# Short experts' fold matmuls move into the Else arm of the branch around the third passes (one core, mixture-of-experts trunk)

## The chip, the cores and the metric

The kernel runs on one core of one Trainium2 chip. The metric is the device time of one execution in microseconds (us), lower is better. The figure before is 1691.68 us, the median of 3 runs (1690.11 to 1696.17).

## What is computed

The reference is a two-layer trunk over 256 tokens of width 1024: an RWKV-7 time mix with a dense feed-forward part, then an attention layer with a mixture of experts (MoE), and a final norm. The change lies in the mixture of experts alone:

```python
# 8 experts, the best 2 of them per token; x is [256, 1024], w_gu[e] is [1024, 2*3584], w_down[e] is [3584, 1024]
gate, up = jnp.split(x @ w_gu[e], 2, axis=-1)
y_e = (jax.nn.silu(gate) * up) @ w_down[e]        # for the tokens routed to expert e
out[token] += gate_weight[token, e] * y_e
```

All is float32. The weights of one expert are 44 MB, and all 8 experts are read.

## The kernel before

**Float32 by passes.** A float32 weight tile `raw` of 128 x 2048 is split into two fp32r tiles: `wh` is its rounded value (line 214, a cast on ScalarE, ACT in the rows), `wl` the rest (line 215, a subtraction on VectorE, DVE). The tokens are split in the same way, into `xgh` and `xgl`. A product is made of three passes of matmuls: `wh` with `xgh`, `wl` with `xgh`, and the third, `wh` with `xgl`.

**Short and long experts.** An expert works on a tile of 128 token slots. If at most 64 tokens were routed to it, it is called short here: then the upper 64 slots of `xgh` hold the low parts of the same tokens, so that the first two passes compute the third one as well, in rows 64 to 127 of the result. The third passes are left out, and a "fold" adds the second half of the rows to the first: ACT copies the psum bank `pgu` into `gc`, times `mode.short`, which is 1 or 0 (line 1538), and TensorE (PE) multiplies `gc` by the constant `fold`, a shifted identity, and accumulates into the same bank (`mm`, line 1503). If more than 64 tokens were routed to it (long), the third passes are done; the fold is done too, with a `gc` that is all zeros. The choice is a branch on PE alone, on the register `mode.many`, once for each pair of weight tiles (line 1527).

**Order of work.** The 7168 gate and up columns are walked in chunks of 1024, 1024, 1024 and 512 columns; each chunk has a gate half and an up half, and each half is some pairs of weight tiles: `pair(...)` issues `two(0)` (8 matmuls of 128 x 512), the branch around `third()` (8 matmuls), hooks, `two(1)` (8 matmuls), hooks. An expert has 14 such pairs for gate and up and 7 for the down product. Each half of a chunk has one fold for each of its banks, 14 in an expert. They are issued one pair late, as the first work after the branch of the first pair of the next half: the folds of a gate half in `first_half`, ahead of the Silu (line 1553), those of an up half in `second_half`, ahead of the product of gate and up (line 1560). Transposes (line 1565) and the split of the hidden values into `hx` follow one pair later. A scheduler of the framework writes the order of each engine's instructions; it may put other matmuls that are ready between the folds, and folds ahead of matmuls that are not. `scatter` (lines 1604 to 1606) adds an expert's output to `res` while the next expert begins.

**Buffers and queues.** Weights come in 1 MB transfers into 7 `raw` buffers, issued in turn from two queues (SP and POOL); a `raw` buffer is free again after its subtraction on DVE. There are 4 `wh` and 3 `wl` buffers. `wh` of a pair's first tile is last read by `third()`, so its buffer is free when the branch is over. In the arm in which `third()` is skipped, PE raises the semaphore by itself with an EVENT_SEMAPHORE instruction.

```python
W.get()                      # splits up to two tiles ahead of the pair in work
nc.scalar.copy(hi, src)                                          # line 214, ACT
nc.vector.tensor_tensor(lo, src, hi.bitcast(F32), ALU.subtract)  # line 215, DVE
```

The functions that the change touches:

Of the kernel before, what the change touches and what calls it, by code (L numbers as in the profile page):

```python
# [106 lines left out]
def tile_trunk(ctx: ExitStack, tc: tile.TileContext, x, norm_g, final_g, mu, w_rkv, w0, w1, w2, a0, a1, a2,  # L107
               g1, g2, k_k, k_a, r_k, gn_g, gn_b, w_o, f_w_in, f_bf, f_qg, f_kg, f_wo, ff_gu, ff_dn,
               m_wr, m_gu, m_dn, cst, out, stages=("rwkv", "ffn", "fox", "moe", "fin")):
# [7 lines left out]
    def ps(name="ps"):  # L117
        return psum.tile([128, 512], F32, name=name, tag="ps")
# [94 lines left out]
    def split(src, hi, lo):  # L213
        nc.scalar.copy(hi, src)  # L214
        nc.vector.tensor_tensor(lo, src, hi.bitcast(F32), ALU.subtract)  # L215
# [1153 lines left out]
    def moe(W, npool, mpool, norm, last_stats):  # L1369
# [17 lines left out]
        for t in range(2):  # L1387
            p = ps("plg")
# [15 lines left out]
        p = ps("pp0")  # L1404
# [8 lines left out]
        for hf in range(2):  # L1413
            cs = slice(hf * 512, (hf + 1) * 512)
            p = ps("pgb")
# [28 lines left out]
        p = ps("pcn")  # L1444
# [57 lines left out]
        def mm(o, l, r, first=False, last=False):  # L1502
            nc.tensor.matmul(o, l, r, start=first, stop=last, skip_group_check=True)  # L1503

        def pair(W, mode, blocks, lhs, out, hooks):


            ws = [W.get() for _ in range(2)]

            def two(i):  # L1510
                for part in range(2):
                    for ti, j, k in blocks:
                        if ti == i:
                            for b, o in enumerate(out):
                                mm(o, lhs(k)[0], ws[i][part][:, j, b * 512:(b + 1) * 512], part == 0 and k == 0,
                                   part == 1 and i == 1)

            def third():
                for ti, j, k in blocks:
                    for b, o in enumerate(out):  # L1520
                        mm(o, lhs(k)[1], ws[ti][0][:, j, b * 512:(b + 1) * 512])

            two(0)
            if mode.many is None:
                third()
            else:
                with tc.If(mode.many > 64):
                    third()
            for f in hooks[0]:
                f()  # L1530
            two(1)
            for f in hooks[1]:
                f()
# [4 lines left out]
            nc.scalar.activation(gc, p, AF.Copy, scale=mode.short)  # L1538
            return lambda: mm(p, fold, gc, last=True)

        def up_chunk(c, W, g, i, mode, todo):

            n0, w = CH[c]
            nb, a = w // 512, 2048 // w
            todo = list(todo)
            pgu, sgs, folds = [], [], []

            def first_half():
                for b in range(nb):
                    folds[b]()  # L1550
                for b in range(nb):
                    sg = spool.tile([128, 512], F32, name="sg", tag="xn")
                    nc.scalar.activation(sg, pgu[0][b], AF.Silu)
                    sgs.append(sg)

            def second_half():
                for b in range(nb):
                    folds[b]()
                for b in range(nb):
                    nc.vector.tensor_tensor(sgs[b], sgs[b], pgu[1][b], ALU.mult)  # L1560

            def transposes(b):
                p = ps("pht")
                for j in range(4):
                    nc.tensor.transpose(p[:, j * 128:(j + 1) * 128], sgs[b][:, j * 128:(j + 1) * 128], ident)
                p = p.rearrange("p (j t) -> p j t", j=4)
                h, l = hidden(n0 // 512 + b)
                nc.scalar.copy(h[:, :, 0:64], p[:, :, 0:64])
                nc.scalar.activation(h[:, :, 64:128], p[:, :, 64:128], AF.Copy, scale=mode.other)  # L1569
                nc.vector.tensor_tensor(l, p, h.bitcast(F32), ALU.subtract)  # L1570
                nc.vector.scalar_tensor_tensor(h[:, :, 64:128], l[:, :, 0:64].bitcast(F32), mode.short,
                                               h[:, :, 64:128].bitcast(F32), ALU.mult, ALU.add)

            for gu in range(2):
                p = [ps("pgu") for _ in range(nb)]
                pgu.append(p)
                n = KB // a // 2
                for q in range(n):
                    blocks = [(ti, j, (q * 2 + ti) * a + j) for ti in range(2) for j in range(a)]
                    hooks = [todo.pop(0) if todo else [] for _ in range(2)]  # L1580
                    if gu == 1 and q == 0:
                        hooks[0] = [first_half] + hooks[0]
                    pair(W, mode, blocks, lambda k: (g[1][:, k, i, :], g[2][:, k, i, :]), p, hooks)
                folds = [folded(x, b, mode) for b, x in enumerate(p)]
            return [[second_half], []] + [[lambda b=b: transposes(b)] for b in range(nb)]

        def down(W, mode, todo):
            acc = [ps("acc") for _ in range(2)]
            todo = list(todo)
            for q in range(7):  # L1590
                blocks = [(ti, j, (q * 2 + ti) * 2 + j) for ti in range(2) for j in range(2)]
                hooks = [todo.pop(0) if todo else [] for _ in range(2)]
                pair(W, mode, blocks, lambda f: (hh[f // 4][:, f % 4, :], hl[f // 4][:, f % 4, :]), acc, hooks)
            return acc

        def scatter(acc, ohT, i, gcol):
            y = [npool.tile([128, 2, 512], F32R, name="y", tag=f"u32{nh}") for nh in range(2)]
            for nh in range(2):
                split(acc[nh], y[nh][:, 0], y[nh][:, 1])
            for t in range(2):  # L1600
                for nh in range(2):
                    cs = slice(nh * 512, (nh + 1) * 512)
                    p = ps("psc")
                    nc.tensor.matmul(p, ohT[:, i, t, :], y[nh][:, 0], start=True, stop=False)
                    nc.tensor.matmul(p, ohT[:, i, t, :], y[nh][:, 1], start=False, stop=True)
                    nc.vector.scalar_tensor_tensor(res[t][:, cs], p, gcol(t), res[t][:, cs], ALU.mult, ALU.add)


        hh, hl = [], []
# [25 lines left out]
        modes = [Mode(cnt[:, 0, e:e + 1], cnt[:, 1, e:e + 1]) for e in range(E)]  # L1635
        with tc.high_priority(offset=AHEAD):
            g = gather([pcol(0), pcol(1)], modes[0:2])
        todo = [[gates]]
        for e in range(E):
            mode = modes[e]  # L1640
            mode.many = nc.values_load(cnti[0:1, e:e + 1], engines=(mybir.EngineType.PE,), min_val=0, max_val=T)
            for c in range(len(CH)):
                todo = up_chunk(c, W, g, e % 2, mode, todo)
            nxt = {}
            if e % 2 == 1 and e + 1 < E:
                todo.append([lambda: nxt.update(g=gather([pcol(e + 1), pcol(e + 2)], modes[e + 1:e + 3]))])
            acc = down(W, mode, todo)
            todo = [[lambda acc=acc, o=g[0], e=e: scatter(acc, o, e % 2, lambda t: gate[:, t, e:e + 1])]]
            g = nxt.get("g", g)
            if e == 0:  # L1650
                top = most()
# [8 lines left out]
        with tc.If(top > 127):  # L1660
            with tc.For_i(0, E, 1) as e:
                pick = rot.tile([128, 2, E], F32, name="pick")
                prod = rot.tile([128, 2, E], F32, name="prod")
                pg = rot.tile([128, 2, 2], F32, name="pg")
                for t in range(2):
                    nc.vector.tensor_scalar(pick[:, t, :], cc("iota", 0, E), ec, None, ALU.is_equal)
                for i, src in ((0, pos), (1, gate)):
                    nc.vector.tensor_tensor(prod, pick, src, ALU.mult)
                    nc.vector.tensor_reduce(pg[:, i, :], prod, AX.X, ALU.add)
                nc.vector.tensor_scalar(ec, ec, 1.0, None, ALU.add)  # L1670
                nc.vector.tensor_scalar(pg[:, 0, :], pg[:, 0, :], 128.0, None, ALU.subtract)
                always = Mode(cc("iota", 0, 1), cc("ones", 0, 1))
                g = gather([lambda t: pg[:, 0, t:t + 1]], [always])
                dyn = lambda w: w[0, bass.ds(e, 1)].rearrange("o d n -> (o d) n")
                W2 = Weights([wraw] * NRA + [mob] * NRB, W.sp, expert_specs(dyn(m_gu), dyn(m_dn)), 2)
                todo = []
                for c in range(len(CH)):
                    todo = up_chunk(c, W2, g, 0, always, todo)
                scatter(down(W2, always, todo), g[0], 0, lambda t: pg[:, 1, t:t + 1])
            last_stats()  # L1680
        es.close()

# [16 lines left out]
    W = Weights([wraw] * NRA, wsp, specs, 2)  # L1699
# [33 lines left out]
    if "fin" in stages:  # L1733
        gains = []
        for hf in range(2):
            p = ps("pfg")
# [42 lines left out]
```

## Time and profile before

| | |
|---|---|
| median of 3 runs | 1691.68 us (1690.11 to 1696.17) |
| the profiled execution | 1692.88 us, span 1691.0 us |
| busy, share of the span | PE 92%, DVE 77%, ACT 65%, POOL 10% |
| mean granted PE clock | 0.958 of full speed |
| experts 0 to 7 | about 713 to 1672 us of the span |
| fold matmuls | 112, 50.7 us busy |
| copies into `gc` | 112, 72.3 us busy |

Spans and stretches are microseconds from the span's start. The three experts with third passes are 2, 3 and 7; 0, 1, 4, 5 and 6 are short. A matmul's busy time is longer than the distance between the starts of two matmuls, because they are pipelined.

### The profile page before, as it was taken

Reading aid. Unit: us, or ns where it says so; the run is one execution under the profiler, and the core shown is the slowest. Engines: PE = TensorE matmul, PEld = TensorE weight load, DVE = VectorE, ACT = ScalarE, POOL = GpSimd, SP = SyncE. Lnnn points to the kernel's source line nnn. Section 1 sums busy time; section 2 is a strip of 40 time slices with the busy share of each in tenths; the row PEclk is TensorE's granted clock in tenths of the full one; section 3 lists DMA queues with packets and bytes.
Section 4 is the critical chain, followed back from the end, with each engine's and each line's share of the span. In section 5 each row is a group of like instructions: output and inputs, shape, how many; then the busy total and the mean of one; then the engine's idle time right before and its main releaser. Section 6 shows DMA issues by size and latency. Waiting matters only on the chain. (4 is left out here: it accounts for less than half of the span.)

```text
span 1691.0 us, 20004 instructions
## 1 busy us (share of the span) xinstructions
PE 1555.7 (92%) x7275; PEld 1201.5 (71%) x7275; DVE 1297.7 (77%) x1357; ACT 1106.7 (65%) x1148; POOL 176.7 (10%) x230
## 2 busy tenths in 40 slices
PE   5998998999999999998889999999988889888996
PEld 4655876888888887766566788788665567566885
DVE  5587557555546556699899888888899899998985
ACT  4633245444435665598688777677788798797783
POOL 0412010000000000011111111110111111111110
PEclk9998598999999999799899999999999999999999
DMA  5233133555555442579899999899899999999982
GB/s 178 88 109 104 22 106 132 189 180 199 183 193 181 150 150 100 224 297 384 347 397 370 364 357 362 327 358 341 312 387 397 360 401 370 382 383 368 373 338 84
DMA packets 156816, 445.73 MB, mean 264 GB/s; under 512 B 24129, under 2 KB 29425, under 8 KB 156705
## 3 DMA queue, kind: packets, MB, share of 16 engines
q1 hardware_dynamic: 105440, 262.95, 42.4%
q0 software_dynamic: 45920, 176.31, 27.5%
q10 hardware_dynamic: 5344, 5.01, 1.0%
q8 instruction: 67, 1.10, 0.3%
q14 instruction: 45, 0.36, 0.1%
HBM read 442.12 MB, written 2.11 MB: 263 GB/s over the span
## 5 line engine op out<-in xcount | busy, mean ns | idle before, releaser
L215 DVE TENSOR_TENSOR wl<-raw,wh 128x2048 fp32r<-128x2048 f32 x398 | 890.6, 2284 | 108.9 <-PE acc L219 35.3
L214 ACT CAST wh<-raw 128x2048 fp32r<-128x2048 f32 x398 | 752.6, 1914 | 304.4 <-PE pgu L220 51.4
L1503 PE MATMUL pgu<-wh,xgh 128*128 128x512 f32 x896 | 259.7, 408 | 10.5 <-ACT wh L214 3.9
L1503 PE MATMUL pgu<-wl,xgh 128*128 128x512 f32 x896 | 252.3, 403 | 13.7 <-DVE wl L215 13.7
L1503 PEld LDWEIGHTS pgu<-wh,xgh 128*128 128x128 f32 x896 | 169.5, 195 | 64.1 <-issue 22.5
L1503 PEld LDWEIGHTS pgu<-wl,xgh 128*128 128x128 f32 x896 | 171.7, 193 | 54.4 <-DVE wl L215 18.0
L1503 PE MATMUL acc<-wh,hx 128*128 128x512 f32 x616 | 165.2, 399 | 5.2
L180 POOL DMA_DIRECT2D raw<-in_moe_w_gu_dram x112 | 79.9, 714 | 668.7 <-DVE wl L215 556.4
L1503 PEld LDWEIGHTS acc<-wh,hx 128*128 128x128 f32 x616 | 113.3, 189 | 41.3 <-issue 12.7
L1503 PE MATMUL acc<-wl,hx 128*128 128x512 f32 x448 | 127.3, 402 | 3.0 <-DVE wl L215 2.1
L1503 PEld LDWEIGHTS acc<-wl,hx 128*128 128x128 f32 x448 | 82.2, 189 | 28.9 <-DVE wl L215 11.5
L218 PE MATMUL pgu<-wh,uh 128*128 128x512 f32 x224 | 89.3, 399 | 1.9 <-ACT wh L214 1.9
L219 PE MATMUL pgu<-wl,uh 128*128 128x512 f32 x224 | 88.2, 394 | 1.6 <-DVE wl L215 1.6
L220 PE MATMUL pgu<-wh,ul 128*128 128x512 f32 x224 | 88.2, 394 | 0.0
L1503 PE MATMUL pgu<-wh,xgl 128*128 128x512 f32 x336 | 85.0, 395 | 0.0
L1503 PE MATMUL pgu<-gc,fold 128*128 128x512 f32 x112 | 50.7, 464 | 37.1 <-ACT gc L1538 35.4
L1503 PEld LDWEIGHTS pgu<-wh,xgl 128*128 128x128 f32 x336 | 63.1, 188 | 14.9
L1538 ACT ACTIVATE gc<-pgu,cnt 128x512 fp32r<-128x512 f32 x112 | 72.3, 692 | 1.3 <-PE pgu L1503 1.3
L180 POOL DMA_DIRECT2D raw<-in_moe_w_down_dram x56 | 39.4, 704 | 294.8 <-DVE wl L215 165.2
L1503 PEld LDWEIGHTS pgu<-gc,fold 128*128 128x128 f32 x112 | 21.1, 189 | 64.0 <-ACT gc L1538 60.3
L1570 DVE TENSOR_TENSOR hx<-pht,hx 128x512 fp32r<-128x512 f32 x56 | 37.3, 689 | 32.2 <-ACT hx L1569 32.2
L219 PEld LDWEIGHTS pgu<-wl,uh 128*128 128x128 f32 x224 | 42.8, 191 | 10.7 <-DVE wl L215 2.0
(366 smaller groups left out, 2185.2 us busy)
## 6 DMA issues: line engine op xcount, KB each, us to landing
raw<-in_moe_w_gu_dram SPq DMA_DIRECT2D x112, 1024.0 KB, 9.6
raw<-in_moe_w_gu_dram POOLq DMA_DIRECT2D x112, 1024.0 KB, 9.7
raw<-in_moe_w_down_dram SPq DMA_DIRECT2D x56, 1024.0 KB, 8.9
raw<-in_moe_w_down_dram POOLq DMA_DIRECT2D x56, 1024.0 KB, 8.6
raw<-in_ffn_w_gu_dram SPq DMA_DIRECT2D x28, 1024.0 KB, 5.4
raw<-in_fox_w_in_dram SPq DMA_DIRECT2D x16, 1024.0 KB, 5.7
raw<-in_ffn_w_down_dram SPq DMA_DIRECT2D x14, 1024.0 KB, 4.9
raw<-in_rwkv_w_rkv_dram SPq DMA_DIRECT2D x24, 512.0 KB, 4.4
```

Source lines behind the costliest of these rows:

```text
L180: (nc.gpsimd if self.nd >= N_EARLY and self.nd % 2 else nc.sync).dma_start(t, src)
L214: nc.scalar.copy(hi, src)
L215: nc.vector.tensor_tensor(lo, src, hi.bitcast(F32), ALU.subtract)
L218: nc.tensor.matmul(o, lh, rh, start=first, stop=False)
L219: nc.tensor.matmul(o, lh, rl, start=False, stop=False)
L220: nc.tensor.matmul(o, ll, rh, start=False, stop=last)
L1503: nc.tensor.matmul(o, l, r, start=first, stop=last, skip_group_check=True)
L1538: nc.scalar.activation(gc, p, AF.Copy, scale=mode.short)
L1570: nc.vector.tensor_tensor(l, p, h.bitcast(F32), ALU.subtract)
```

## The change

The folds no longer stand in `first_half` and `second_half`. They are handed to the first pair of the next half and stand there in the Else arm of the branch on `mode.many`: a short expert executes its folds in that arm, a long one executes `third()` and no fold. The copies into `gc` stay for both. Nothing else is altered but the passing of the list.

```diff
-        def pair(W, mode, blocks, lhs, out, hooks):
+        def pair(W, mode, blocks, lhs, out, hooks, folds=()):
...
-                with tc.If(mode.many > 64):
+                with tc.If(mode.many > 64) as arm:
                     third()
+                if folds:
+                    with arm.Else():
+                        for f in folds:
+                            f()
             for f in hooks[0]:
                 f()
             two(1)
...
             def first_half():
-                for b in range(nb):
-                    folds[b]()
                 for b in range(nb):
                     sg = spool.tile([128, 512], F32, name="sg", tag="xn")
                     nc.scalar.activation(sg, pgu[0][b], AF.Silu)
                     sgs.append(sg)
 
             def second_half():
-                for b in range(nb):
-                    folds[b]()
                 for b in range(nb):
                     nc.vector.tensor_tensor(sgs[b], sgs[b], pgu[1][b], ALU.mult)
...
-                    pair(W, mode, blocks, lambda k: (g[1][:, k, i, :], g[2][:, k, i, :]), p, hooks)
+                    pair(W, mode, blocks, lambda k: (g[1][:, k, i, :], g[2][:, k, i, :]), p, hooks, folds if q == 0 else ())
                 folds = [folded(x, b, mode) for b, x in enumerate(p)]
-            return [[second_half], []] + [[lambda b=b: transposes(b)] for b in range(nb)]
+            return [[second_half], []] + [[lambda b=b: transposes(b)] for b in range(nb)], folds
```

`down` takes the last folds of an expert in the same way, for its first pair. A fallback for experts with more than 128 tokens loses its folds; it does not run with these inputs.

## Rows read from the trace of the kernel before

**Rows 1.** Busy time of each engine in the stretch of one expert: experts 2 and 3 (long), 4 and 6 (short), 7 (long). Columns: from and to, length, then busy us (and instructions) of PE, PE's weight loads, DVE, ACT and POOL, granted PE clock, busy share of the DMA engines, GB/s.

```profile
938.00:1064.50 126.50, 124.30 (x554) 101.17 (x553) 110.67 (x71) 96.59 (x80) 15.62 (x22) 1.00 0.93 361
1064.50:1200.00 135.50, 133.11 (x619) 109.58 (x618) 112.62 (x83) 103.83 (x90) 14.92 (x21) 1.00 0.89 335
1200.00:1313.00 113.00, 98.89 (x392) 70.39 (x390) 107.19 (x69) 93.82 (x79) 14.92 (x21) 0.97 0.97 373
...
1430.00:1541.00 111.00, 97.47 (x387) 68.90 (x386) 105.81 (x69) 93.28 (x79) 14.91 (x21) 0.97 1.00 387
1541.00:1672.00 131.00, 126.32 (x560) 101.84 (x558) 108.66 (x71) 93.89 (x80) 12.81 (x18) 1.00 0.80 308
```

**Rows 2.** The matmuls of the third passes (tile `xgl`) in the stretches of experts 2 and 4; columns as in rows 1, of these instructions alone (PE, weight loads, ACT).

```profile
938.00:1064.50 126.50, 28.32 (x112) 21.03 (x112) 0.00 (x0) 1.00 0.93 361
...
1200.00:1313.00 113.00, 0.00 (x0) 0.00 (x0) 0.00 (x0) 0.97 0.97 373
```

**Rows 3.** The stretches of two long experts, 2 and 7, after their first chunk's gate half; columns as in rows 1.

```profile
960.00:1064.50 104.50, 104.50 (x472) 85.78 (x471) 93.50 (x59) 80.68 (x68) 13.50 (x19) 1.00 0.96 369
...
1566.00:1672.00 106.00, 105.55 (x476) 86.31 (x474) 89.21 (x58) 76.37 (x66) 10.71 (x15) 1.00 0.78 300
```

**Rows 4.** The folds (tile `fold`) in the same two stretches: PE, weight loads, DVE.

```profile
960.00:1064.50 104.50, 4.40 (x12) 2.25 (x12) 0.00 (x0) 1.00 0.96 369
...
1566.00:1672.00 106.00, 4.40 (x12) 2.25 (x12) 0.00 (x0) 1.00 0.78 300
```

**Rows 5.** Timeline of PE at one pair of folds in long expert 7: start, length, instruction, count.

```profile
1573.73 2.02 PE L1503 MATMUL pgu<-wh,xgl 128*128 128x512 f32 x8
1575.59 0.40 PE L1503 MATMUL pgu<-gc,fold 128*128 128x512 f32 x1
1575.82 0.39 PE L1503 MATMUL pgu<-wh,xgh 128*128 128x512 f32 x1
1576.05 0.39 PE L1503 MATMUL pgu<-gc,fold 128*128 128x512 f32 x1
```

**Rows 6.** Timeline of PE behind the folds of the first gate half of long experts 2, 3 and 7; in brackets the idle time before and what ended it.

```profile
956.56 1.20 PE L1503 MATMUL pgu<-wl,xgh 128*128 128x512 f32 x4 [1.10 <-DVE wl L215]
...
1083.38 0.96 PE L1503 MATMUL pgu<-wl,xgh 128*128 128x512 f32 x3 [2.31 <-DVE wl L215]
...
1561.69 1.20 PE L1503 MATMUL pgu<-wl,xgh 128*128 128x512 f32 x4 [2.31 <-DVE wl L215]
```

**Rows 7.** Waits between 938 and 1200 us (long experts 2 and 3): who waited, for whom, us in total, times, longest.

```profile
ACT wh L214 <- PE pgu L1503: 20.3, 25, 2.2
ACT wh L214 <- PE acc L1503: 20.2, 15, 2.2
```

**Rows 8.** Waits between 1200 and 1541 us (short experts 4, 5 and 6).

```profile
ACT wh L214 <- PEq L1527: 28.4, 26, 3.4
PE pgu L1503 <- ACT gc L1538: 24.5, 24, 2.7
DVE res L1606 <- PE psc L1605: 11.5, 3, 6.0
ACT wh L214 <- DMA raw<-in_moe_w_gu_dram: 9.2, 13, 1.4
ACT wh L214 <- DMA raw<-in_moe_w_down_dram: 7.4, 9, 1.9
DVE hx L1570 <- ACT hx L1569: 7.0, 6, 2.1
```

**Rows 9.** The stretches of short experts 4 and 6 behind their first chunk; columns as in rows 1.

```profile
1225.00:1313.00 88.00, 77.31 (x312) 55.01 (x312) 85.21 (x55) 74.70 (x64) 12.10 (x17) 0.98 1.01 393
...
1450.00:1541.00 91.00, 80.97 (x321) 57.01 (x321) 88.37 (x56) 76.95 (x66) 12.80 (x18) 0.96 1.01 390
```

**Rows 10.** What PE's sequencer executed for line 1527, the branch: count, shortest, median and longest (ns), first and last start.

```profile
L1527 PEldq COMPARE_BRANCH  x231: 65/179/353, 712.9 to 1665.5; - x116
L1527 PEldq EVENT_SEMAPHORE  x105: 51/51/51, 715.2 to 1540.3; - x105
```

**Rows 11.** Timeline in short expert 4, from a branch without folds behind it to one with folds behind it.

```profile
1243.45 1.08 PE L1503 MATMUL pgu<-wl,xgh 128*128 128x512 f32 x4
1244.65 0.76 PEld L1503 LDWEIGHTS pgu<-wh,xgh 128*128 128x128 f32 x4 [0.55 <-issue]
1244.68 1.16 PE L1503 MATMUL pgu<-wh,xgh 128*128 128x512 f32 x4
...
1249.06 0.50 PE L1503 MATMUL pgu<-gc,fold 128*128 128x512 f32 x1 [1.41 <-ACT gc L1538]
1249.39 0.39 PE L1503 MATMUL pgu<-wh,xgh 128*128 128x512 f32 x1
1249.49 3.71 ACT L214 CAST wh<-raw 128x2048 fp32r<-128x2048 f32 x2
...
1249.64 0.50 PE L1503 MATMUL pgu<-gc,fold 128*128 128x512 f32 x1
```

**Rows 12.** Timeline in short expert 4 at the folds of the first gate half.

```profile
1211.17 6.69 DVE L215 TENSOR_TENSOR wl<-raw,wh 128x2048 fp32r<-128x2048 f32 x3
1211.25 1.18 ACT L1553 ACTIVATE sg<-pgu 128x512 f32<-128x512 f32 x2
...
1214.82 3.75 ACT L214 CAST wh<-raw 128x2048 fp32r<-128x2048 f32 x2 [2.39 <-PEq L1527]
```

More of the change, by code (lines that the diff above doesn't have):

```diff
@@ L1539, in folded, with up_chunk @@
             return lambda: mm(p, fold, gc, last=True)
-        def up_chunk(c, W, g, i, mode, todo):
+        def up_chunk(c, W, g, i, mode, todo, folds):
             n0, w = CH[c]
@@ L1545, in up_chunk @@
             todo = list(todo)
-            pgu, sgs, folds = [], [], []
+            pgu, sgs = [], []
             def first_half():
-                for b in range(nb):
-                    folds[b]()
                 for b in range(nb):
@@ L1582, in up_chunk, with down @@
                         hooks[0] = [first_half] + hooks[0]
-                    pair(W, mode, blocks, lambda k: (g[1][:, k, i, :], g[2][:, k, i, :]), p, hooks)
+                    pair(W, mode, blocks, lambda k: (g[1][:, k, i, :], g[2][:, k, i, :]), p, hooks, folds if q == 0 else ())
                 folds = [folded(x, b, mode) for b, x in enumerate(p)]
-            return [[second_half], []] + [[lambda b=b: transposes(b)] for b in range(nb)]
-        def down(W, mode, todo):
+            return [[second_half], []] + [[lambda b=b: transposes(b)] for b in range(nb)], folds
+        def down(W, mode, todo, folds):
             acc = [ps("acc") for _ in range(2)]
@@ L1592, in down @@
                 hooks = [todo.pop(0) if todo else [] for _ in range(2)]
-                pair(W, mode, blocks, lambda f: (hh[f // 4][:, f % 4, :], hl[f // 4][:, f % 4, :]), acc, hooks)
+                pair(W, mode, blocks, lambda f: (hh[f // 4][:, f % 4, :], hl[f // 4][:, f % 4, :]), acc, hooks,
+                     folds if q == 0 else ())
             return acc
@@ L1637, in moe @@
             g = gather([pcol(0), pcol(1)], modes[0:2])
-        todo = [[gates]]
+        todo, folds = [[gates]], []
         for e in range(E):
@@ L1642, in moe @@
             for c in range(len(CH)):
-                todo = up_chunk(c, W, g, e % 2, mode, todo)
+                todo, folds = up_chunk(c, W, g, e % 2, mode, todo, folds)
             nxt = {}
@@ L1646, in moe @@
                 todo.append([lambda: nxt.update(g=gather([pcol(e + 1), pcol(e + 2)], modes[e + 1:e + 3]))])
-            acc = down(W, mode, todo)
+            acc = down(W, mode, todo, folds)
+            folds = []
             todo = [[lambda acc=acc, o=g[0], e=e: scatter(acc, o, e % 2, lambda t: gate[:, t, e:e + 1])]]
@@ L1675, in moe @@
                 W2 = Weights([wraw] * NRA + [mob] * NRB, W.sp, expert_specs(dyn(m_gu), dyn(m_dn)), 2)
-                todo = []
+                todo, folds = [], []
                 for c in range(len(CH)):
-                    todo = up_chunk(c, W2, g, 0, always, todo)
-                scatter(down(W2, always, todo), g[0], 0, lambda t: pg[:, 1, t:t + 1])
+                    todo, folds = up_chunk(c, W2, g, 0, always, todo, folds)
+                scatter(down(W2, always, todo, folds), g[0], 0, lambda t: pg[:, 1, t:t + 1])
             last_stats()
```

## The prediction

> **What bounds the kernel now.** The page comes first: PE is busy 92% of the span and DVE 77%, but these are means over stages with different limits, so the next view is the windows, one for each expert [rows 1]. The reader is to see two regimes. Experts 2, 3 and 7 take 126.5 to 135.5 us, experts 4 and 6 only 111 to 113 us. Which are long is told by the third passes: 112 matmuls with `xgl` in the window of expert 2 and none in that of expert 4 [rows 2]; with 56 matmuls of the down product in each that is 21 pairs of 8.
>
> Long experts, behind their first gate half, are PE's: 104.5 of 104.5 us busy at full clock, with DVE at 93.5 us and the DMA engines at a share of 0.96, or 0.78 in expert 7 [rows 3]. The waits say the same from the other side: ACT, which makes `wh`, waits there for matmuls, 20.3 and 20.2 us [rows 7]. Whatever PE need not do in these stretches should come off the time, as long as DVE and the transfers keep up. DVE's 93.5 of 104.5 us leaves room for some 11 us an expert.
>
> Short experts are not PE's. Behind the first chunk the DMA share is 1.01 and DVE is busy 85.21 of 88 us and 88.37 of 91 us, 97%, against 88 to 89% for PE [rows 9]. DVE's larger waits are for the scatter's matmuls (11.5 us in three experts) and for `hx` (7.0 us), and ACT waits for transfers in 22 places, 16.6 us [rows 8]. So weights arrive no faster than they are eaten there, and PE has idle time: 24.5 us in three experts waiting for `gc` alone [rows 8].
>
> **The change part by part.** *Folds that go away.* A long expert loses its 14 folds, 42 in all. What one costs is not its busy time but what it takes from the row of matmuls: in the timeline the starts of a fold, a `wh` matmul and the next fold lie 0.23 us apart, 1575.59, 1575.82, 1576.05, and the first fold stands straight behind the third passes without a wait [rows 5]. 12 of the 14 lie in the stretch in which PE never rests [rows 4]: 12 x 0.23 x 3 = 8.3 us. The other two stand in the first gate half, and behind them PE waits 1.10 to 2.31 us for `wl` in all three experts [rows 6]: without them it waits longer, so they give nothing. If they did: 14 x 0.23 x 3 = 9.7 us. The bounds are 0, if DVE were the true limit, and 9.7; I take 8.3, since DVE has four times that room in each expert.
>
> The Trainium skill, "TensorE: Matmul & The Clock Gate", section "Wait — 56ns, not 53.3ns?", gives 215.7 ns from start to start for 512 columns at the full clock. The trace agrees within 7%; an estimate from that page would be 36 x 0.2157 = 7.8 us instead of 8.3.
>
> *Folds that move into the arm.* A short expert has 8 first pairs with folds (7 halves and the first pair of the down product), 40 places in five experts. The folds keep their number and their wait for `gc`. What moves is the end of the branch. The sequencer's rows show 231 compare-and-branch instructions and 105 events [rows 10]: 168 branches, 63 jumps (3 long experts x 21 pairs), and 5 x 21 = 105 events, one for each skipped third pass. So an Else arm exists already and no branch is added. The event costs PE something: behind it the weight load comes 0.55 us after the one before ended and the matmul at 1244.68, while the fourth matmul before it started at about 1243.45 + 3 x 0.23 = 1244.14; that is 0.54 us instead of 0.23, or 0.31 us lost [rows 11]. I read it as PE emptying before the event is raised. At the places with folds this loss lies before today, inside the wait for `gc` (1.41 us at 1249.06 [rows 11]), and costs nothing. In the arm the event has to come behind the folds, in the open: 0.31 us, and up to 0.23 us more where a `wh` matmul now fills the time between two folds (1249.39 between 1249.06 and 1249.64 [rows 11]). So 40 x 0.31 = 12.4 to 40 x 0.54 = 21.6 us of PE time, about 17.
>
> The same event lets ACT go on. The cast behind `gc` starts at 1249.49 today; if it needs the buffer that this branch holds, it can start only when the second fold is done, 1249.64 + 0.50 = 1250.14, so 0.65 us later [rows 11]. Queued behind it on ACT is the next cast, then DVE's subtraction waits for it, and behind that the `raw` buffer and the transfer on SP or POOL.
>
> How much of the 17 us comes through? What covers it is the transfers: at a share of 1.01 a weight that is split half a microsecond later delays nothing while other transfers are queued, and DVE at 97% has work waiting [rows 9]. 35 of the 40 places lie there. If that cover were gone, all of 21.6 us would show. The other five lie in the first chunk. There the folds run ahead of PE's wait for `wl` today and the two Silus at 1211.25 right behind them; in the arm they come after it, and the cast at 1214.82 may queue behind the Silus, 1.18 us more [rows 12]. DVE has three subtractions in hand at that point (6.69 us from 1211.17, to 1217.9 [rows 12]), so this too is mostly hidden. Bounds 0 and 21.6 us. The nearest rows, the DMA share and DVE's, speak for the low end; I take a quarter of 17 us, 4 us.
>
> *What costs nothing.* The copies into `gc` stay, so ACT's work is the same. In long experts the Silu now waits for the end of the branch; ACT has 24 us of idle time there (80.68 of 104.5 us busy [rows 3]).
>
> **The sum**, against the profiled execution's own 1692.88 us: 1692.9 - 8.3 + 4 = 1688.6. The median of the runs is 1.2 us below that execution, so 1687.4 us. A change of this kernel under 0.5%, 8.5 us, is about what a measurement can't tell from none: faster means below 1683.2, slower above 1700.1.
>
> **The rivals.**
> *Faster: the order of PE's work gets better in short experts.* The scheduler handles both arms as one block, which isn't ready before `gc` is; it may put the 8 matmuls of `two(1)` ahead of the block, and the wait for `gc` disappears behind them. It is 24.5 us in three experts [rows 8], 41 us in five, and with a quarter coming through 10 us: 1691.7 - 8.3 - 10 = 1673. For it: folds and other matmuls are mixed already [rows 11]. Against it: PE isn't what short experts wait for, and a later end of the branch keeps ACT waiting, which waits for branches 28.4 us already [rows 8]. If only the cost in short experts is nothing, it is 1683.4, at the edge.
> *Slower: PE and ACT turn in a loop in short experts* (end of branch, cast, `gc`, fold, end of branch), and the later event goes round with it. For it: ACT's 28.4 us of waiting for branches is its largest wait [rows 8]. Against it: the 22 waits for transfers, in which such a delay is lost. In full it is 1691.7 - 8.3 + 21.6 = 1705; it decides from about three quarters of 21.6 on.
> *Slower: the waits stand before the branch.* If the wait for `gc` were placed ahead of the compare, long experts would still wait for two copies at each of 24 places. A wait like that of 1249.06, 1.41 us [rows 11], at 24 places is 34 us; the third passes then start late, and with 8.3 us won it is 1717. Nothing in the rows speaks for it but that the arm is one block.
> *Slower: the code of the arm isn't there in time.* Then entering the Else arm would stall as long again as the 0.55 us behind the event [rows 11], 40 x 0.55 = 22 us, 1705 if none is hidden. The arms stand already, and their jumps show 0.55 us, event included. The Trainium skill, "Runtime: NRT & Kernel Launch", section "Instruction fetch mechanics", says that a taken branch whose target lies outside the pages at hand stalls until they are fetched; by that rule a longer arm could stall where a short one doesn't, and no row here shows such a fetch.
> *No change: the long experts give nothing*, because DVE or the transfers take over at once: 1691.7. Against it: rows 3.
>
> **How the numbers follow.** My forecast 0.52; order gets better 0.24; loop 0.12; waits before the branch 0.04; code late 0.02; nothing from long experts 0.06. So faster 0.24, same 0.52 + 0.06 = 0.58, slower 0.18. The range for 8 in 10 begins a little into the faster case, at 1678, as the whole 9.7 us and a third of the better order's 10 us would give, and reaches up to 1702, most of the way to the loop's 1705.
>
> **What would show each step.** Right: 70 folds instead of 112; long stretches still without idle PE and each about 2.8 us shorter; in short experts the event behind the folds, the load after it about 0.55 us later, and short stretches within 1 us of before. Wrong: long experts as long as before with a wait of PE for `wl` or `gc` in them; short experts longer by 2 us or more each with a DMA share below 1.0; or short experts clearly shorter with fewer waits for `gc`.

## The result, and the profile after

The kernel after runs in 1683.67 us (median; 1678.15 to 1696.86), the kernel before beside it on the same chip in 1696.07 us: a ratio of 0.9936, 95% interval [0.9916, 0.9956]. That is faster by 7.5 to 14.2 us, 10.9 in the middle, where the prediction had 4.3 us and called "no change" the likeliest. A second comparison on another occasion gave 0.9956 [0.9925, 0.9987]. The profiled execution took 1688.97 us, span 1687.2.

The groups of the page that the change touches. Columns: busy us, mean ns, then the idle time before them and what ended it.

```profile
PE 1543.0 (91%) x7233; PEld 1197.3 (71%) x7233; DVE 1297.7 (77%) x1357; ACT 1106.3 (66%) x1148; POOL 176.4 (10%) x230
L1543 ACT ACTIVATE gc<-pgu,cnt 128x512 fp32r<-128x512 f32 x112 | 73.1, 694 | 4.1 <-PE pgu L1503 4.0
L1503 PE MATMUL pgu<-gc,fold 128*128 128x512 f32 x70 | 31.9, 481 | 32.1 <-ACT gc L1543 31.7
```

The folds are 70 as foreseen, the copies into `gc` still 112, and PE still waits 31.7 us for them. What the sequencer executed for the branch, now line 1528 (compare [rows 10]):

```profile
L1528 PEldq COMPARE_BRANCH  x231: 65/179/350, 712.2 to 1662.0; - x116
L1528 PEldq EVENT_SEMAPHORE  x65: 51/51/51, 714.5 to 1538.5; - x65
```

As many branches as before, but 65 events instead of 105: the 40 places with folds have none any more.

Long experts behind their first gate half, experts 2 and 7 (columns as in rows 1; then the folds alone: PE, weight loads, DVE):

```profile
960.00:1064.00 104.00, 103.97 (x469) 85.14 (x468) 93.10 (x58) 83.22 (x71) 13.17 (x19) 1.00 0.97 374
1564.00:1668.00 104.00, 103.97 (x468) 84.84 (x466) 88.84 (x56) 77.39 (x68) 10.66 (x15) 1.00 0.81 305
```
```profile
960.00:1064.00 104.00, 0.00 (x0) 0.00 (x0) 0.00 (x0) 1.00 0.97 374
1564.00:1668.00 104.00, 0.00 (x0) 0.00 (x0) 0.00 (x0) 1.00 0.81 305
```

PE still has no rest there, and the 12 folds [rows 4] are gone: the stretch is as [rows 3] with less in it.

Two profiled executions can't be compared by their spans: the part ahead of the MoE, the same code in every kernel here, took 702.0 to 719.5 us in 13 profiles. So all kernels are compared by stages, each from the first `psc` matmul of one scatter to that of the next (expert 0 from its first matmul with `xgh`), read from PE's timelines. Sums in us; "first gate halves" run from that matmul to the start of the third passes of the long expert's fifth pair.

| kernel | long experts (2, 3, 7) | of it first gate halves | of it the rest | short experts (5) | ratio to before |
|---|---|---|---|---|---|
| before | 382.6 | 76.7 | 305.9 | 576.3 | |
| before, another execution | 388.7 | 82.8 | 305.9 | 574.2 | 1.0004 [0.9979, 1.0028] |
| after | 379.5 | 81.3 | 298.3 | 576.6 | 0.9936 [0.9916, 0.9956] |
| after, another execution | 379.5 | 81.2 | 298.3 | 577.4 | 0.9956 [0.9925, 0.9987] |
| long_only | 381.5 | 84.2 | 297.3 | 577.0 | 0.9955 [0.9928, 0.9983] |
| short_only | 384.1 | 78.2 | 305.9 | 574.2 | 0.9989 [0.9962, 1.0015] |
| first_back | 376.8 | 79.6 | 297.2 | 576.1 | 0.9940 [0.9910, 0.9969] |
| sag_pad | 374.0 | 76.7 | 297.3 | 577.0 | 0.9937 [0.9913, 0.9961] |
| arm_early | 371.8 | 73.6 | 298.2 | 577.5 | 0.9889 [0.9850, 0.9927] |
| short_pad | 378.8 | 81.3 | 297.5 | 566.5 | 0.9873 [0.9835, 0.9912] |
| gc_first | 381.1 | 82.9 | 298.2 | 564.2 | 0.9883 [0.9836, 0.9930] |
| before_gc | 402.7 | 86.0 | 316.7 | 564.3 | 1.0039 [1.0006, 1.0071] |
| gc_first_early | 371.8 | 73.5 | 298.3 | 563.2 | 0.9818 [0.9772, 0.9864] |

The rest of the long experts hardly varies: 305.9 in three profiles of kernels that keep all folds in place, 297.2 to 298.3 where the folds are gone. The first gate halves don't repeat, and that is the second story below. Between the two profiles first shown, the long experts lost 3.1 us, the short ones gained 0.3, and 1.0 lies in the parts before and behind the MoE.

PE in the first gate half of expert 2, before (straight behind the first line of [rows 6]), and then after:

```profile
957.59 2.03 PE L1503 MATMUL pgu<-wh,xgl 128*128 128x512 f32 x8
959.46 1.07 PE L1503 MATMUL pgu<-wh,xgh 128*128 128x512 f32 x4
```

```profile
950.75 1.09 PE L1503 MATMUL pgu<-wh,xgh 128*128 128x512 f32 x4
955.04 2.07 PE L1503 MATMUL pgu<-wl,xgh 128*128 128x512 f32 x4 [3.20 <-DVE wl L215]
956.91 2.67 PE L1503 MATMUL pgu<-wh,xgl 128*128 128x512 f32 x8
959.42 1.07 PE L1503 MATMUL pgu<-wh,xgh 128*128 128x512 f32 x4
```

The wait for `wl` is one of 3.20 us now. The four matmuls that follow take 2.07 us instead of 1.20 [rows 6], and the eight third passes 2.67 us, where eight of them at full clock take 2.02 [rows 5]. The windows of that place show why (the column behind POOL is the granted clock):

```profile
956.00:958.50 2.50, 2.50 (x8) 1.92 (x7) 2.50 (x2) 0.00 (x0) 0.70 (x1) 0.53 0.23 28
959.00:962.00 3.00, 3.00 (x15) 2.48 (x14) 3.00 (x3) 3.00 (x4) 0.71 (x1) 1.00 1.00 407
```

0.53 is close to the lower level, 1.2 GHz, right after 3.20 us in which PE did nothing; from 959 on it is 2.4 GHz again. Ten microseconds around the same place in the other long experts (1077:1087 and 1554:1564) show a mean of 0.83 each.

### The profile page after: what moved, and what is told of

The parts are those of the page before. It is cut to its first block, busy times and chain, and to the rows that moved or that the text cites. A ratio compares the mean times of both kernels' runs of the same rounds, so it can differ in the third digit from the quotient of the medians.

```text
span 1687.2 us, 19952 instructions
## 1 busy us (share of the span) xinstructions
PE 1543.0 (91%) x7233; PEld 1197.3 (71%) x7233; DVE 1297.7 (77%) x1357; ACT 1106.3 (66%) x1148; POOL 176.4 (10%) x230
## 5 line engine op out<-in xcount | busy, mean ns | idle before, releaser
L1503 PE MATMUL pgu<-wl,xgh 128*128 128x512 f32 x896 | 256.1, 406 | 24.2 <-DVE wl L215 24.0
L1503 PE MATMUL pgu<-wh,xgh 128*128 128x512 f32 x896 | 255.1, 406 | 14.2 <-ACT wh L214 9.1
L1503 PEld LDWEIGHTS pgu<-wl,xgh 128*128 128x128 f32 x896 | 171.4, 194 | 67.4 <-DVE wl L215 31.7
L1503 PE MATMUL pgu<-gc,fold 128*128 128x512 f32 x70 | 31.9, 481 | 32.1 <-ACT gc L1543 31.7
L1572 DVE TENSOR_TENSOR hx<-pht,hx 128x512 fp32r<-128x512 f32 x56 | 37.2, 691 | 28.4 <-ACT hx L1571 27.8
L1503 PEld LDWEIGHTS pgu<-gc,fold 128*128 128x128 f32 x70 | 14.1, 201 | 50.7 <-issue 40.0
```

## The experiments

**Each part alone.** In long_only the kernel before keeps its order, and the folds of the long experts, known from this input, are left out of the program, those of the short ones stay behind the branch:

```diff
-                for b in range(nb):
+                for b in range(nb if mode.fold else 0):     # fold = e not in (2, 3, 7)
                     folds[b]()
```

> The kernel before, with the folds of experts 2, 3 and 7 left out where the program is written (their copies are zeros, so the result is the same), and everything in the short experts as before: no Else arm. Theory A: 8.3 us less than before, ratio 0.995. Theory B: 3 us less, ratio 0.998, since the idle time in the first gate half is longer here too; then the short experts must hold the other 8 us of the measured 11. Theory D (the whole gain comes from the long experts): 11 us, ratio 0.9935.

In short_only the long experts run their folds behind the branch, and only the short experts have them in the arm:

```diff
-                if folds:
+                if folds and mode.arm:                      # arm = e not in (2, 3, 7)
                     with arm.Else():
...
+                if not mode.arm:
+                    for f in folds:
+                        f()
```

> The folds stand in the Else arm for the five short experts alone; experts 2, 3 and 7 do theirs behind the branch as before. Theory A: 4 us more than before, ratio 1.0024. Theory B: 8 us less, ratio 0.995. Theory D: no difference, 1.000.

Beside them after once more:

> The changed kernel once more, for a second profile. The runs say 0.9936 of before (11 us), the two profiles only 3.9 us: by stage, 3.1 us in the three long experts and 0.2 us in the five short ones. Theory A (as predicted): long experts 8.3 us shorter in all, short ones 4 us longer. Theory B: long experts are only about 3 us shorter in all, because without the two folds of the first gate half PE idles longer there and its clock falls (3.20 us idle and third passes of 2.67 instead of 2.02 us in the first profile). Theory C: that fall of the clock is an accident of this one execution, and in others the long experts are some 8 us shorter. A second profile with the clock at 1.00 in the ten microseconds behind that idle time speaks for C, one at 0.83 to 0.88 for B.

Measured: long_only 0.9955 [0.9928, 0.9983], short_only 0.9989 [0.9962, 1.0015], after 0.9956 [0.9925, 0.9987]. The gain is that of the long experts; the arm in the short ones costs or gives nothing that can be measured, in ratio as in stages (574.2 and 577.0 us, in a spread of 574.2 to 577.5 for kernels with and without it).

**The two folds of the first gate half.** first_back puts those two of the 14 back behind the branch in long experts, in front of the wait for `wl`:

```diff
+                if mode.first:                              # long expert, first chunk, first pair of the up half
+                    for f in folds:
+                        f()
```

> The changed kernel, but the two folds of the first gate half of each long expert stand where they stood before, ahead of the wl matmuls for which PE waits there; 6 folds more than the changed kernel. Theory B: PE's clock stays at 1.00 behind that place, and the kernel is 3 to 5 us faster than the changed one, ratio to before about 0.991. Theory C and D: as the changed kernel, 0.9936, within 2 us.

sag_pad is first_back with these folds issued six times, which keeps PE at work through nearly all of the wait (`gc` is zero in a long expert):

```diff
-                    for f in folds:
+                    for f in folds * 6:
```

> The changed kernel, but in the first gate half of each long expert the two folds stand ahead of the wl matmuls as before and are issued six times over (their gc is zeros), 12 matmuls of 0.23 us into PE's wait for wl. Theory B (the wait without work lets PE's clock fall, which costs about 1.5 us a place): no slow third passes in any of the three places, first-half stretches 25.3 to 25.9 us as before instead of 26.9 to 27.3, the long experts about 375 us in sum. Rival (the longer stretch comes from a wait of ACT or DVE, not from the clock): stretches of 26.9 us or more also with PE kept busy.

And the kernel before against itself, for the clock in its first gate halves:

> The kernel before against itself: ratio 1.000. How far it lies from that tells what the comparison is worth. Its second profile gives the stages once more: if the three long experts come to 382.6 us as in the first, the 3.1 us that the changed kernel's two profiles win there are sure; if PE's clock falls in a first gate half here too, they come out up to 1.5 us longer for each such place.

PE at the same place of expert 2 in sag_pad, and the granted clock there:

```profile
944.22 3.06 PE L1504 MATMUL pgu<-gc,fold 128*128 128x512 f32 x12
947.45 1.18 PE L1504 MATMUL pgu<-wl,xgh 128*128 128x512 f32 x4 [0.18 <-DVE wl L215]
948.47 2.02 PE L1504 MATMUL pgu<-wh,xgl 128*128 128x512 f32 x8
```
```profile
948.00:951.00 3.00, 3.00 (x14) 2.44 (x13) 3.00 (x2) 1.56 (x2) 0.70 (x1) 1.00 0.21 34
```

The `wl` matmuls start 4.3 us behind the `wh` matmuls at 943.16 in this kernel, and 4.3 us behind those at 950.75 in after (955.04): 12 useless matmuls cost nothing, and the work behind them runs at full clock. Windows of 3 us along all first gate halves, from the `psc` matmul on, give the count of places where the granted clock fell: 15 of 15 where the two folds are missing (after twice, long_only, short_pad, gc_first), 6 of 12 where they stand (before none of 3, before again all 3, short_only 1, first_back 2), none of 3 in sag_pad; in before_gc, with a rest of 2.73 us, it fell at 2 of 3. The first gate half takes 25.3 to 25.9 us without a fall and 26.6 to 28.3 with one; two of the 15, in expert 7 of long_only and gc_first, take 30.1 and 28.9 us, and there the clock had fallen once before the wait too. In ratio first_back (0.9940) and sag_pad (0.9937) don't stand apart from after; stages show this effect, the timed runs don't resolve it.

arm_early fills that wait with work there is anyway: in this one pair the branch, and so the third passes, which need `wh` alone, goes ahead of the `wl` matmuls.

```diff
-            two(0)
+            two(0, [0] if early else range(2))              # early: first chunk, first pair of the up half
             ...                                             # the branch with third passes and folds
+            if early:
+                two(0, [1])
```

> The changed kernel, but in the first pair of each expert's first up half the branch (third passes or folds) stands ahead of the wl matmuls of two(0). There PE waits 3.2 us for wl in the long experts; the 8 matmuls of the third passes, 1.86 us, need only wh and fill that wait. Theory B: 1.9 us for each long expert and the fall of the clock, 1.5 us, gone: long experts about 10 us shorter in sum than in the changed kernel, 369 to 371 us; ratio to before about 0.988. Rival (DVE, late by the scatter's adds, sets the end of this stretch): long experts as in the changed kernel, 379.5 us.

```profile
941.83 1.10 PE L1503 MATMUL pgu<-wh,xgh 128*128 128x512 f32 x4
942.76 2.02 PE L1503 MATMUL pgu<-wh,xgl 128*128 128x512 f32 x8
946.12 1.19 PE L1503 MATMUL pgu<-wl,xgh 128*128 128x512 f32 x4 [1.33 <-DVE wl L215]
```

The wait shrinks from 3.20 to 1.33 us, the third passes take 2.02 us, no clock falls in any of the three experts, and the first gate halves take 73.6 us instead of 81.3: 2.6 us an expert. The long experts come to 371.8 us, a little above the 369 to 371 expected, and the ratio to 0.9889 [0.9850, 0.9927].

**The arm in short experts, tripled.** short_pad has two matmuls by a zero matrix behind each fold of the arm, so that PE does three times the work there and the branch ends later:

```diff
                         for f in folds:
                             f()
+                            f(zero)
+                            f(zero)
```

> The changed kernel with two more matmuls behind each fold in the Else arm, by a matrix of zeros, so that they add nothing: 140 matmuls of 0.23 us in the short experts, 32 us of PE time, and the end of the branch 0.5 to 0.9 us later at each of 40 places. Theory cover (transfers and DVE set the pace of short experts): at most 5 us more than the changed kernel. Theory loop (PE and ACT wait for each other through the end of the branch): 32 us more, ratio to before about 1.013. The prediction's quarter: 8 us.

Nothing that was expected came: 0.9873 [0.9835, 0.9912], and the short experts take 566.5 us, ten less than after, with more work on PE. The waits of experts 4 to 6 in after, and in short_pad (who waited, for whom, us in total, times, longest):

```profile
PE pgu L1503 <- ACT gc L1543: 20.2, 17, 2.1
ACT wh L214 <- PEq L1528: 14.2, 19, 2.0
```
```profile
ACT wh L214 <- PEq L1530: 6.0, 11, 0.9
PE pgu L1505 <- ACT gc L1547: 2.8, 8, 0.5
```

PE's wait for `gc` is gone. It isn't the padding as work that does this, but what it did to the program: the order of the instructions on ACT is fixed when the program is built, and with a longer arm it came out differently. Between two branches ACT has two casts (`wh`) and, where a half ended, the copies into `gc`. Counted in ACT's timelines, both casts stand ahead of the copy at 108 of 112 places in before, at 76 in after and at 40 in short_pad. So the change had moved 32 places by itself, and the short experts had gained nothing measurable from these; which of the places matter wasn't followed. What the order costs is seen in the timeline of after, expert 4:

```profile
1237.46 1.92 ACT L214 CAST wh<-raw 128x2048 fp32r<-128x2048 f32 x1 [0.52 <-PEq L1528]
1240.11 1.90 ACT L214 CAST wh<-raw 128x2048 fp32r<-128x2048 f32 x1 [0.73 <-DMA raw<-in_moe_w_gu_dram]
1241.91 1.26 ACT L1543 ACTIVATE gc<-pgu,cnt 128x512 fp32r<-128x512 f32 x2
```
```profile
1238.44 2.32 PE L1503 MATMUL pgu<-wl,xgh 128*128 128x512 f32 x8
1242.74 0.98 PE L1503 MATMUL pgu<-gc,fold 128*128 128x512 f32 x2 [1.98 <-ACT gc L1543]
```

The second cast waits for its transfer, the copy is queued behind it, PE waits 1.98 us for the copy, and the matmuls that would free the next buffers wait with it.

**That order by itself.** gc_first is after with one rule more: of the two casts traced in a pair with folds, the second is queued behind the last copy into `gc`. No work is added.

```diff
-            ws = [W.get() for _ in range(2)]
+            ws = [W.get()]
+            with tc.issue_after(mode.last.ins) if folds else ExitStack():   # last: the last copy into gc
+                ws.append(W.get())
```

> The kernel after, with one rule of order more on ACT and no other work: of the two casts (`wh`) that stand between two branches where `gc` is made, the second is queued behind the two copies into `gc`. After has one cast ahead of 36 of the 112 copies in the program and two ahead of 76; short_pad had one ahead of 72; here one stands ahead of all 112. Theory E (the gain of short_pad in short experts was this order, not the padding): PE's wait for `gc`, 6 to 7 us in each of experts 4, 5 and 6, falls to about 1 us, and the five short experts take 563 to 569 us instead of 576 to 577; ratio to before 0.986 to 0.990. Theory F (the padding did it, by keeping PE at work or by a later end of the branch): the order alone gives nothing, short experts 574 to 578 us, ratio 0.993 to 0.997.

before_gc has the same rule in the kernel before:

> The kernel before, with the same rule of order on ACT and without the change. Theory E: the wait for `gc` is ACT's order in either kernel, so short experts fall by about 10 us here too, to 564 to 569 us, long ones stay at 383 to 389 us, ratio 0.993 to 0.995. If the folds have to stand in the arm for that order to pay (F, or both needed): short experts 573 to 578 us, ratio 0.998 to 1.002.

Measured: gc_first 0.9883 [0.9836, 0.9930], short experts 564.2 us; before_gc 1.0039 [1.0006, 1.0071], short experts 564.3 us but long ones 402.7. The same three experts in gc_first wait less than half as long for `gc`:

```profile
PE pgu L1503 <- ACT gc L1545: 7.3, 7, 1.3
ACT wh L214 <- PEq L1530: 4.6, 8, 1.3
```

That is 2.4 us an expert, where about 1 was expected. Of the 12.9 us that PE waits less for `gc` in these three, 7.7 come off their time (347.3 to 339.6 us).

Theory E holds: the order alone, in either kernel, makes the short experts 10 to 14 us shorter (10 to 12 in before_gc, 12 to 13 in gc_first, 14 from arm_early to gc_first_early). What nobody foresaw is the price in the kernel before, here at a pair of folds in its long expert 2:

```profile
1019.50 1.92 ACT L214 CAST wh<-raw 128x2048 fp32r<-128x2048 f32 x1 [0.67 <-PE pgu L1503]
1022.33 0.69 ACT L1541 ACTIVATE gc<-pgu,cnt 128x512 fp32r<-128x512 f32 x1 [0.91 <-PE pgu L1503]
1022.92 1.90 ACT L214 CAST wh<-raw 128x2048 fp32r<-128x2048 f32 x1
1023.07 0.50 PE L1503 MATMUL pgu<-gc,fold 128*128 128x512 f32 x1 [0.84 <-ACT gc L1541]
```

A long expert's half ends just before the copy can start, so ACT stands idle for 0.91 us and PE for 0.84, for a fold that adds zeros; the rest of the three long experts takes 316.7 us instead of 305.9. With the change no matmul of a long expert reads `gc`, and the rest stays at 298.2. So the order pays only together with the change.

**Both.** gc_first_early joins gc_first and arm_early.

> arm_early (in the first pair of each second gate half the branch stands before the `wl` matmuls of `two(0)`) and the order of gc_first together. If the two gains are of different places they add up: long experts 371 to 373 us as in arm_early, short experts 563 to 569 us by theory E, ratio 0.980 to 0.985. By F, or if the one order spoils the other: ratio as arm_early alone, 0.988 to 0.991.

0.9818 [0.9772, 0.9864], 1666.0 us against 1691.61 us of before: long experts 371.8 us, short ones 563.2. The two gains are of different places and add up; this version beats both kernels.

## Why the prediction was right or wrong

*The time* was within the range, 3.7 us below the point, with a kernel before that ran 4.4 us slower beside it than in the three runs the forecast starts from. The gain was 4.3 us foreseen and 10.9 [7.5, 14.2] measured. The bound of "no change", 8.5 us, lies inside that interval, and the second comparison (7.5 us in the middle) lies on its other side, so these runs don't decide between the "no change" that I had given 0.58 and a small "faster". What I called the edge, the cost in short experts being nothing, is the case that came.

*Folds that go away: right.* 8.3 us for 36 folds in stretches without rest. The rest of the long experts, which holds these 36, gave 7.65 us in after (305.9 to 298.25, 0.21 us a fold) and 8.6 in long_only, first_back and sag_pad (0.24). The difference is one group of eight `wh` matmuls an expert that takes 2.29 us in after and 1.98 in sag_pad; why it does wasn't followed. The Trainium skill's start-to-start time ("TensorE: Matmul & The Clock Gate", section "Wait — 56ns, not 53.3ns?"), 7.8 us for 36, lies between the two, so these runs decide nothing between that figure and the row's 0.23.

*"Without them it waits longer, so they give nothing": the step that failed.* The wait did grow so that the next matmuls start no earlier (4.3 us behind the `wh` matmuls with or without anything in it). But I priced a wait as empty time. After 3.20 us of rest in one piece the granted clock stood near half, and the 12 matmuls behind took 1.48 us more: 1.87 instead of 1.03 us from the start of the four `wl` matmuls to that of the third passes, 2.51 instead of 1.87 us for these, against the kernel before at 956.56 to 959.46. Three such places took 4.6 us between the two profiles shown (first gate halves 76.7 to 81.3), more than half of the folds' gain. That pair flatters the kernel before, in which the clock falls at times too, though PE rests only 2.0 to 2.3 us behind the folds: on average a first gate half takes 27.39 us without the folds (15 places; 27.07 without the two with an earlier fall) and 26.44 with them (12), so the removal costs 2 to 3 us in three experts. It is a rough mean: the sum for three experts is 76.7 to 82.8 us in the four profiles that keep the folds.

*The cost in short experts, +4 us: not there.* The bound 0 was right, but for another reason than the cover of DMA and DVE. I had the event come behind the folds; the profile shows 65 events, none at the 40 places. The arm's own last matmul seems to release what waits for the branch: in experts 4 to 6 ACT's waits for events fell from 28.4 [rows 8] to 14.2 us and those for PE's matmuls rose from 4.8 to 17.8, so the sum hardly moved. The second of these, before and after:

```profile
ACT wh L214 <- PE pgu L1503: 4.8, 5, 1.9
...
ACT wh L214 <- PE pgu L1503: 17.8, 11, 4.8
```

In the timeline of after the folds stand in the row like any matmuls:

```profile
1219.80 1.08 PE L1503 MATMUL pgu<-wl,xgh 128*128 128x512 f32 x4
1220.71 0.64 PE L1503 MATMUL pgu<-gc,fold 128*128 128x512 f32 x2
1221.20 1.09 PE L1503 MATMUL pgu<-wh,xgh 128*128 128x512 f32 x4
```

From 1219.80 to 1221.20 lie 1.40 us for six matmuls, 0.23 each: no stall on either side. The price that I read from [rows 11] is one of arms that are empty. short_pad, which tripled the arm without harm, agrees that no time hangs on its length.

*The rivals.* The loop of PE and ACT, at 1705, is refuted by short_only and short_pad. Waits ahead of the branch: long experts show none for `gc` in their busy stretches. Code that comes late: compare-and-branch takes 179 ns in the median and 350 at most, as before [rows 10]; the Trainium skill's fetch stall ("Runtime: NRT & Kernel Launch", section "Instruction fetch mechanics") doesn't show with the longer arm. No gain in long experts: refuted by the 7.65 us. The faster rival, a better order in short experts, did not happen in after, where PE still waits 20.2 us for `gc` in experts 4 to 6 (24.5 before [rows 8]). But its worth was real: gc_first got about 13 us from it, on ACT, not on PE as I had put it. My argument against it, that PE isn't what short experts wait for, was wrong: their waits for `gc` are on the path, since a late fold holds the end of the half and with it the buffers.

*Luck.* Folds 7.65, the clock -2 to -3, short experts 0: stages explain some 5 us. That this lies near the 4.3 of the sum is luck: a cost of 4 us that wasn't there stood in it for one of 2 to 3 that I hadn't foreseen.

*What stays open.* Timed runs show 7.5 to 14.2 us in one comparison and 2.2 to 12.7 in the other. Every run lists its mean granted clock, and the time of one kernel follows it: in 85 runs of before, with clocks from 0.950 to 0.967, the correlation is -0.87. A straight line through these and 33 runs of after gives 1.2 us for each 0.001 and, at the same clock, 5.5 us (95%: 4.4 to 6.7) between the two kernels, near what the stages give. The rest of the gain goes with the clock of the runs, 0.9585 in the mean in before and 0.9610 in after. In the profiles it is the part ahead of the MoE whose length follows its clock: it takes 704.1 us at a mean of 0.96 (sag_pad) and 719.5 us at 0.93 (gc_first_early). Why the runs of after had the higher clock isn't shown.

## What to carry to other kernels

Work taken out of a stretch in which an engine never rests comes off the time at its start-to-start price; work taken out of a wait of TensorE can cost, because here the longer rest was followed by a slower clock, so fill such a wait with work that is due anyway (arm_early) before emptying it. A short copy that TensorE waits for shouldn't be queued on its engine behind a long one that waits for a transfer: read the order of that engine's queue whenever such a wait shows, since it can change with any edit, even one that adds only useless work. And test each part alone: here an order that was worth 10 to 12 us in one kind of expert cost more than that in the other until the change had taken away its reader.

## What the runs showed of the hardware that was not expected

After a rest of 3.20 us TensorE ran at a granted clock of 0.53, near 1.2 GHz, and was back at 1.00 some 3 us later. After shorter rests the same program went either way: in experts 3 and 7 of the kernel before, PE rested 2.31 us in both profiles, and the clock stayed at 1.00 in one and fell in the other. Twelve matmuls on zeros, 3.06 us, kept it at 1.00 and cost no time. And the arms that do matmuls had no event instruction for what waits behind them, where an empty arm has one and, as I read it, 0.31 us of TensorE's time with it [rows 10, 11].
